# A hybrid encoder layer on one core: 192 instead of 128 tokens gathered, queries in two passes, one-hots in bf16

## The chip, the core and the metric

The kernel runs on one core of a Trainium2 chip. The metric is the device time of one execution in microseconds (us), lower is better. Engines are named as in the profile: PE is the matrix engine and PEld its weight loads, DVE the vector engine, ACT the scalar engine, POOL the GpSimd engine, SP the engine whose queue issues most loads. The core has 16 DMA engines that all queues share.

## What is computed

One layer over 512 tokens of width 2048: a normed input projection, two kinds of attention, an output projection with a residual, and then a channel mixer that retrieves single neurons. The change lies in the output projection's tail and in the mixer, which is, cut to what matters:

```python
qry = (xt @ w_query).reshape(T, 8, 2, 128)
sc = einsum('thcd,hckd->thck', qry, sub_keys)          # 2 x 128 scores per token and head
top_s, top_i = top_k(sc, 16)
cand_s = top_s[:, :, 0, :, None] + top_s[:, :, 1, None, :]
cand_i = top_i[:, :, 0, :, None] * 128 + top_i[:, :, 1, None, :]
best_s, best_pos = top_k(cand_s, 16)                   # 16 of 256 pairs
idx, gates = take(cand_i, best_pos), softmax(best_s)   # 8 heads x 16 = 128 neurons a token
act = gelu(sum_d(expert_down[idx] * xt))
out = sum_k(gates * act * expert_up[idx])              # 16384 neurons, rows of 2048 floats
```

## The kernel before

Tokens of the mixer are treated in two ways. For the first 384 (`DENSE`) all 16384 neurons are computed as matrix products, 128 groups `e` of 128 neurons, and the gates of the neurons not chosen are zero. For the other 128 tokens, one on each partition, the chosen rows of the two tables are gathered by indirect DMA, one row of 8 KB per token and slot, 128 slots for each table.

Every product in fp32 is made of three matmuls (`mm3`, lines 117 to 120): each operand is split into a high part (`high`, line 69, on ACT) and a rest (`low`, line 77, on DVE or, where the stream says so, on POOL). Weights come through `Stream`: loads of 1 MB on SP's queue, two raw buffers, each load cut into two pieces of 0.5 MB whose halves are made one piece ahead of the matmuls, into three buffers each.

The stages in order are: input projection and attention; the output projection (`out_granule`, line 582), four moving blocks of 384 columns and one of 512 per weight block; the query projection (line 923), eight heads, with two calls of `TopK` per head (lines 786 to 871) dealt out in four pieces each; a tail of 40 steps in which the first products of the mixer run beside the last top-k work; the one-hot stage (line 1043), 96 steps of 4 tokens, in which the gates are spread to a dense matrix: `e` compares (DVE), `eq` is one half times the gate (POOL in three of four steps, else DVE) and the other half copied by ACT, then four fp32 matmuls, then a copy, and the result goes to DRAM; some further products; and the dense stage (line 1176). There, 16 super-blocks of 8 groups `e` alternate between a down phase (two pieces per group) and an up phase (four column blocks `dc` of four pieces). I call a piece with its 24 matmuls a step; `after` (line 1148) is called once per step, 16 times in the first super-block, 26 times in the second and 32 times in each of the other 14, 490 times in all. It first moves the weighting of finished groups on by one operation (`Weighted.step`: a multiply by `rb2` out of PSUM, the gelu, the gate, the split) and then issues the gathers that are due: 257 items over 462 steps. An item is the fetch of the row two items on (POOL, line 1088, three buffers) and one DVE instruction on the row that has come: a multiply and sum in the first half (line 1096), a multiply and add in the second (line 1106). Each queue works in the order in which the program issues.

Of the kernel before, what the change touches and what calls it, by code (L numbers as in the profile page):

```python
# [21 lines left out]
S = 512  # L22
# [3 lines left out]
DENSE = 384  # L26
DB = DENSE // 128
# [70 lines left out]
def layer(ctx, tc, A, out_t, out_g):  # L98
# [107 lines left out]
    with ExitStack() as st:  # L206
# [268 lines left out]
        with ExitStack() as s2:  # L475
# [179 lines left out]
            o = [pj() for _ in range(5)]  # L655
# [10 lines left out]
    rb2 = gn.tile([128, DENSE], F32, name="rb2")  # L666
    rg = gn.tile([128, 1], F32, name="rg")
    xhl = pool(ctx, "xhl", side="right")
    yh = xhl.tile([128, NT, DENSE], F32R, name="yh")
    yl = xhl.tile([128, NT, DENSE], F32R, name="yl")  # L670
    sg = small.tile([128, 4], F32, name="sg", bufs=1)
    sq = small.tile([128, DENSE], F32, name="sq2", bufs=1)
    nc.gpsimd.dma_start(g2, A["g2"])
    tp2 = pool(out_stage, "tp2")
    xt, xg, x1 = {}, {}, {}

    def fetch(g):
        gs = slice(g * 512, (g + 1) * 512)
        xt[g] = tp2.tile([128, 4, DENSE], F32, name="xt2")
        nc.gpsimd.dma_start(xt[g], A["xT"][:, 4 * g:4 * g + 4, :DENSE])  # L680
        xg[g] = tp2.tile([128, 512], F32, name="xg"), tp2.tile([128, 512], F32, name="g2b")
        nc.gpsimd.dma_start(xg[g][0], A["xg"][:, gs])
        nc.gpsimd.dma_start(xg[g][1], A["g2r"][0:1, gs].to_broadcast([128, 512]))

    def residual(g, o):
        gs = slice(g * 512, (g + 1) * 512)
        x1[g] = tp2.tile([128, 4, DENSE], F32, name="x1")
        for c in range(4):
            nc.vector.tensor_tensor(x1[g][:, c, :], o[c][:, :DENSE], xt[g][:, c, :], op=OP.add)
# [9 lines left out]
    def scaled(dt):  # L699

        x = x1[dt // 4][:, dt % 4, :]
        nc.scalar.activation(yh[:, dt, :], x, AF.Copy, scale=g2[:, dt:dt + 1])
        q = sq if dt == 0 else tp2.tile([128, DENSE], F32, name="q2", bufs=2)
        nc.scalar.square(q, x)
        nc.vector.scalar_tensor_tensor(yl[:, dt, :], x, g2[:, dt:dt + 1], yh[:, dt, :].bitcast(F32),
                                       op0=OP.mult, op1=OP.subtract)
        if dt:
            nc.vector.tensor_tensor(sq, sq, q, op=OP.add)
# [3 lines left out]
    for g in range(1, 4):  # L712
        o = [pj() for _ in range(5)]
# [11 lines left out]
    slot = pool(ctx, "slot", side="right")  # L725
# [556 lines left out]
```

## Time and profile before

| | us |
|---|---|
| median of 3 runs (3424.23 to 3426.03) | 3425.71 |
| the profiled execution, its own time | 3424.43 |
| its span in the trace | 3422.7 |
| PE busy in the span | 3345.8 |
| DVE busy | 2288.5 |
| ACT busy | 1207.6 |
| POOL busy | 790.4 |

The profile gives for each engine its busy time, the instructions of each line with their mean duration, what they waited for, and the clock that PE was granted. Matmuls overlap each other, so the pace of matmuls is read from their starts and not from their durations. DMA is given as the mean busy share of the 16 engines and as GB/s.

### The profile page before, as it was taken

What the parts mean: (1) busy time and instruction counts of PE and PEld (TensorE: products, weight loads), DVE (VectorE), ACT (ScalarE), POOL (GpSimd) and SP (SyncE); (2) the same over time, 40 slices, a digit from 0 to 9 for tenths busy, and PEclk for the clock granted to TensorE, in tenths of its full rate; (3) what the DMA queues carried; (4) which work ended last, traced back from release to release, by engine and by line L of the source; (5) the groups of instructions that cost most, each with busy time, mean ns of one, the idle gap of its engine ahead of it and who ended that gap; (6) DMA issues with size and microseconds to landing.
All of it is one profiled execution on the core that took longest, in us unless ns stands there. A gap on an engine that the chain in (4) does not pass through costs nothing.

```text
span 3422.7 us, 46854 instructions
## 1 busy us (share of the span) xinstructions
PE 3345.8 (98%) x18845; PEld 3179.9 (93%) x18845; DVE 2288.5 (67%) x3660; ACT 1207.6 (35%) x1833; POOL 790.4 (23%) x670
## 2 busy tenths in 40 slices
PE   8999999999988789999999999999999999999999
PEld 6777878799988778999999999999999999999999
DVE  4545353553499996567777777767677777777675
ACT  4334444442222497323223223233232232232332
POOL 3112010100255573012222222222122222222220
PEclk9999999999999999999999999999999999999999
DMA  4222222233312245677777777777787777777775
GB/s 145 87 89 87 86 74 87 87 137 134 125 62 74 81 200 210 237 265 277 284 277 278 276 277 278 271 278 272 263 294 267 278 277 274 276 284 268 278 275 180
DMA packets 146379, 705.65 MB, mean 206 GB/s; under 512 B 11600, under 2 KB 61840, under 8 KB 68336
## 3 DMA queue, kind: packets, MB, share of 16 engines
q1 hardware_dynamic: 99552, 386.82, 32.0%
q0 software_dynamic: 40464, 283.32, 21.9%
q10 hardware_dynamic: 6144, 32.51, 2.4%
q8 instruction: 148, 2.42, 0.3%
q14 instruction: 71, 0.58, 0.1%
HBM read 665.90 MB, written 36.70 MB: 205 GB/s over the span
## 4 chain that ended last, share of the span: by engine, by line
PE 87%; DVE 7%; ACT 4%; issue 1%; DMA 0%; ACTq 0%; SPq 0%; DVEq 0%
PE pj L118 17%; PE pj L119 17%; PE pj L120 17%; PE pa L118 10%; PE pa L120 10%; PE pa L119 10%; ACT eq L1039 2%; PE pa L601 1%; PE pa L540 1%; ACT gs L109 1%; DVE sel L871 1%; PE pa L560 1%; PE pa L911 1%; DVE ti L803 0%; DVE ti L807 0%
## 5 line engine op out<-in xcount | busy, mean ns | idle before, releaser
L77 DVE TENSOR_TENSOR wl2x<-wr4x,wh2x 128x1024 fp32r<-128x1024 f32 x382 | 468.3, 1232 | 372.5 <-ACT wh2x L69 372.2
L118 PE MATMUL pj<-ah,wh2x 128*128 128x384 f32 x2048 | 684.3, 334 | 0.0
L119 PE MATMUL pj<-al,wh2x 128*128 128x384 f32 x2048 | 684.2, 334 | 0.0
L120 PE MATMUL pj<-ah,wl2x 128*128 128x384 f32 x2048 | 684.1, 334 | 0.0
L118 PE MATMUL pa<-yh,wh8x 128*128 128x384 f32 x2000 | 682.6, 341 | 0.0
L120 PE MATMUL pa<-yh,wl8x 128*128 128x384 f32 x2000 | 677.1, 339 | 0.0
L119 PE MATMUL pa<-yl,wh8x 128*128 128x384 f32 x2000 | 677.1, 339 | 0.0
L69 ACT CAST wh2x<-wr4x 128x1024 fp32r<-128x1024 f32 x382 | 400.6, 1049 | 708.7 <-PE pj L119 409.0
L77 DVE TENSOR_TENSOR wl8x<-wr16x,wh8x 128x1024 fp32r<-128x1024 f32 x254 | 312.7, 1234 | 152.8 <-ACT wh8x L69 152.3
L1088 POOL DMA_INDIRECT row<-in_down_dram,idx x128 | 207.2, 1619 | 831.2 <-DVE ga L1096 786.7
L119 PEld LDWEIGHTS pj<-al,wh2x 128*128 128x128 f32 x2048 | 384.4, 188 | 0.0
L120 PEld LDWEIGHTS pj<-ah,wl2x 128*128 128x128 f32 x2048 | 384.4, 188 | 0.0
L118 PEld LDWEIGHTS pj<-ah,wh2x 128*128 128x128 f32 x2048 | 384.4, 188 | 0.0
L1088 POOL DMA_INDIRECT row<-in_up_dram,idx x128 | 207.5, 1621 | 764.2 <-DVE xn L1106 728.8
L118 PEld LDWEIGHTS pa<-yh,wh8x 128*128 128x128 f32 x2000 | 375.5, 188 | 0.0
L119 PEld LDWEIGHTS pa<-yl,wh8x 128*128 128x128 f32 x2000 | 375.5, 188 | 0.0
L120 PEld LDWEIGHTS pa<-yh,wl8x 128*128 128x128 f32 x2000 | 375.3, 188 | 0.1
L69 ACT CAST wh8x<-wr16x 128x1024 fp32r<-128x1024 f32 x256 | 267.0, 1044 | 190.4 <-PE pj L119 81.6
L1200 DVE TENSOR_TENSOR x<-x,pj 128x384 f32<-128x384 f32 x256 | 141.9, 554 | 257.2 <-PE pj L120 257.1
L1106 DVE SCALAR_TENSOR_TENSOR xn<-row,ga,xn 128x2048 f32<-128x2048 f32 x127 | 297.8, 2345 | 0.0
L1096 DVE CUSTOM_DVE_ANT_0 row<-row,xn 128x2048 f32<-128x2048 f32 x128 | 292.3, 2284 | 0.0
L118 PE MATMUL pj<-wh2x,xh 128*128 128x512 f32 x704 | 284.1, 404 | 0.0
(300 smaller groups left out, 4777.3 us busy)
## 6 DMA issues: line engine op xcount, KB each, us to landing
wr16x<-in_downT_dram SPq DMA_DIRECT2D x128, 1024.0 KB, 5.1
wr4x<-in_upT_dram SPq DMA_DIRECT2D x128, 1024.0 KB, 5.5
wr4x<-in_win_dram SPq DMA_DIRECT2D x47, 1024.0 KB, 4.9
gt_d<-gs ACTq DMA_DIRECT2D x12, 2048.0 KB, 6.5
g<-gt_d SPq DMA_DIRECT2D x30, 768.0 KB, 8.6
wr4x<-in_wout_dram SPq DMA_DIRECT2D x16, 1024.0 KB, 4.9
wr8x<-in_wq_dram SPq DMA_DIRECT2D x16, 1024.0 KB, 5.0
xt<-in_xT_dram SPq DMA_DIRECT2D x7, 512.0 KB, 8.5
```

The source lines that it names most:

```text
L69: self.nc.scalar.copy(hi, t)
L77: self.lo_engine[n].tensor_tensor(lo, t, hi.bitcast(F32), op=OP.subtract)
L109: nc.scalar.copy(out, in_)
L118: nc.tensor.matmul(out, sh, mh, start=first, stop=False)
L119: nc.tensor.matmul(out, sh, ml, start=False, stop=False)
L120: nc.tensor.matmul(out, sl, mh, start=False, stop=last)
L540: nc.tensor.matmul(sc[u], qt[:, h, t * 128:(t + 1) * 128], kt[:, h, :], start=True, stop=True)
L1039: nc.scalar.copy(eq[:, 1].rearrange("p t k -> p k t"), e[:, 1])
L1088: nc.gpsimd.indirect_dma_start(out=t, out_offset=None, in_=A["down"] if step < SLOTS else A["up"], in_offset=bass.IndirectOffsetOnAxis(ap= ...
L1096: nc.vector.tensor_tensor_reduce(t, t, xn, 1.0, 0.0, OP.mult, OP.add, ga[:, k:k + 1])
L1106: nc.vector.scalar_tensor_tensor(xn, t, ga[:, k:k + 1], xn, op0=OP.mult, op1=OP.add)
L1200: nc.vector.tensor_tensor(x1[:, dt, :], x1[:, dt, :], o[c], op=OP.add)
```

## The change

The gathered tokens become 192 (`NG`), the dense ones 320. Of the gathered ones, 128 lie one on a partition as before (b = 0); the other 64 are laid on 128 partitions as halves of the width (b = 1): rows of 4 KB, half a table row each, and the two half sums are added by a small matmul (`weights_of_slots`) before the gelu. The gather items become 514, b = 0 and b = 1 in turn, over the same 462 steps. The rests of the weights of the dense stage are made by POOL for 2 pieces of 5 (`lo_share`), by DVE for the others. The norm factor `rb2` moves from the products of each group (line 1126, dropped) into the dense input (`dense_y`); the residual `x1` stays in SBUF and no longer goes through DRAM. The output projection runs with all 512 columns as moving. The queries run in two passes over the same weights, which are loaded and split twice: first the 192 gathered tokens (192 moving columns), then the 320 dense ones; the number of top-k calls stays at 16, four or two heads or token groups packed in one. The last scaling of a top-k call moves from DVE to ACT, the sums of squares from DVE to POOL. In the one-hot stage, now 80 steps, the gate is split in three bf16 parts and the matmuls are 12 in bf16 instead of 4 in fp32; ACT's copy `eq` is dropped, and one `w` of 1536 elements takes the place of an `eq` of 512, on POOL in one of three steps. The diff, cut to its core:

```diff
-DENSE = 384
-DB = DENSE // 128
+NG = 192
+DENSE = S - NG
...
-    for k in range(8):
+    for k in range(16):
         for a in range(0, NT, 8):
-            ws.add(A["wq"][k, :, a:a + 8, :], 2, (nc.gpsimd, nc.gpsimd if k == 0 else None))
+            ws.add(A["wq"][k % 8, :, a:a + 8, :], 2, (nc.gpsimd,))
...
-                        mm3(o[c][:, :DENSE], wh[:, a, cs], wl[:, a, cs], mh[k][:, kk, :DENSE], ml[k][:, kk, :DENSE],
-                            f, l)
-                    mm3(o[4], mh[k][:, kk, DENSE:], ml[k][:, kk, DENSE:], wh[:, a, :], wl[:, a, :], f, l)
+                        mm3(o[c], wh[:, a, cs], wl[:, a, cs], mh[k][:, kk, :], ml[k][:, kk, :], f, l)
...
-        nc.scalar.dma_start(x1_d[:, 4 * g:4 * g + 4, :], x1[g])
+            dt = 4 * g + c
+            nc.vector.tensor_tensor(xq[:, dt, :], o[c][:, DENSE:], xt[g][:, c, DENSE:], op=OP.add)
+            nc.vector.tensor_tensor(x1[:, dt, :], o[c][:, :DENSE], xt[g][:, c, :DENSE], op=OP.add)
...
+        nc.scalar.square(q[:, DENSE:], xq[:, dt, :])
+        nc.scalar.square(q[:, :DENSE], x1[:, dt, :])
...
-            nc.vector.tensor_tensor(sq, sq, q, op=OP.add)
+            nc.gpsimd.tensor_tensor(sq, sq, q, op=OP.add)
...
+
+    def lo_share():
+
+        shares[0] += 1
+        return nc.gpsimd if shares[0] % 5 in (1, 3) else None
...
-        ws.add(A["downT"][e], 2, (nc.gpsimd if e in (1, 2) else None,))
+        ws.add(A["downT"][e], 2, (lo_share(), lo_share()) if e >= PRE else (nc.gpsimd if e in (1, 2) else None,))
...
-                ws.add(A["upT"][sb, dc, :, e:e + 4, :])
+                ws.add(A["upT"][sb, dc, :, e:e + 4, :], 2, (lo_share(), lo_share()))
...
+        def dense_y(dt):
+
+            t = qp.tile([128, DENSE], F32, name="yt", bufs=2)
+            nc.vector.scalar_tensor_tensor(t, x1[:, dt, :], g2[:, dt:dt + 1], rb2[:, :DENSE], op0=OP.mult, op1=OP.mult)
+            nc.scalar.copy(yh[:, dt, :], t)
+            nc.gpsimd.tensor_tensor(yl[:, dt, :], t, yh[:, dt, :].bitcast(F32), op=OP.subtract)
...
-                    nc.vector.tensor_scalar(ge, ge, sm[:, 3 * h + 2:3 * h + 3], None, op0=OP.mult)
+                    nc.scalar.activation(ge, ge, AF.Copy, scale=sm[:, 3 * h + 2:3 * h + 3])
...
+                        mm3(o[c][:, :NG], w[0][:, a, cs], w[1][:, a, cs], zh[:, dt, :], zl[:, dt, :], dt == 0, dt == NT - 1)
...
+                if 1 <= h < 7 and q % 2 == 0 and h * 2 + q // 2 - 2 < 6:
+                    turned_x(h * 2 + q // 2 - 2)
+                if h and q != 1 and (h - 1) * 3 + (q + 1) // 2 < NT:
+                    dense_y((h - 1) * 3 + (q + 1) // 2)
+                pieces(1)
...
+                        mm3(o[c][:, :DENSE], w[0][:, a, cs], w[1][:, a, cs], yh[:, dt, :], yl[:, dt, :], dt == 0, dt == NT - 1)
+                    if q == 0 and a == 1:
+                        scored.one()
+                if q == 0:
+                    scored.two()
+                pieces(2 if q % 2 else 1)
...
-            if n in (7, 12, 20, 28):
+            if n in (7, 12, 18, 22, 26, 30):
...
-            eq = eqs[n] = gp.tile([128, 2, 4, 128], F32, name="eq", bufs=4)
-            (nc.vector if n % 4 == 3 else nc.gpsimd).tensor_tensor(
-                eq[:, 0].rearrange("p t k -> p k t"), e[:, 0], gd[:, ts].unsqueeze(1).to_broadcast([128, 128, 4]), op=OP.mult)
-            nc.scalar.copy(eq[:, 1].rearrange("p t k -> p k t"), e[:, 1])
+            w = gp.tile([128, 3, 128, 4], BF16, name="w", bufs=4)
+            (nc.gpsimd if n % 3 == 2 else nc.vector).tensor_tensor(
+                w, e[:, 0].unsqueeze(1).to_broadcast([128, 3, 128, 4]),
+                gd[:, :, ts].unsqueeze(2).to_broadcast([128, 3, 128, 4]), op=OP.mult)
...
-                nc.tensor.matmul(b[:, u, :], eq[:, 1, u, :], eq[:, 0, u, :], start=True, stop=True)
+                for k in range(3):
+                    nc.tensor.matmul(b[:, u, :], e[:, 1, :, u], w[:, k, :, u], start=k == 0, stop=k == 2)
...
+            fetched[b, step] = t = rows.tile([128, width[b]], F32, name=f"row{b}", bufs=3)
...
+                src = halves[up] if b else A["up" if up else "down"]
+                nc.gpsimd.indirect_dma_start(out=t, out_offset=None, in_=src,
+                                             in_offset=bass.IndirectOffsetOnAxis(ap=idx[b][:, k:k + 1], axis=0))
...
+    def gather(b, step):
+        fetch_rows(b, step + 2)
         k = step % SLOTS
-        t = fetched.pop(step)
...
+            nc.vector.tensor_tensor_reduce(t, t, x, 1.0, 0.0, OP.mult, OP.add, g[:, k:k + 1])
...
+            nc.vector.scalar_tensor_tensor(x, t, g[:, k:k + 1], x, op0=OP.mult, op1=OP.add)
...
-                if self.a is None:
-                    self.a = prep.tile([128, DENSE], F32, name=f"pre{self.e % E}")
-                    nc.vector.tensor_tensor(self.a, self.bank, rb2, op=OP.mult)
-                nc.scalar.activation(self.a, self.a, AF.Gelu_apprx_tanh)
+                src = self.a
+                if src is None:
+                    self.a, src = prep.tile([128, DENSE], F32, name=f"pre{self.e % E}"), self.bank
...
-        while gathered[0] < min(2 * SLOTS + 1, (steps[0] - 16) * 2 * SLOTS // total):
-            gather(gathered[0])
+        if wait_slots[0]:
+            wait_slots[0] -= 1
+            if wait_slots[0] == 0:
+                weights_of_slots()
+            return
+        while gathered[0] < min(END, (steps[0] - 16) * END // total):
+            step, b = divmod(gathered[0], 2)
+            gather(b, step)
             gathered[0] += 1
+            if gathered[0] == 2 * SLOTS:
+                wait_slots[0] = 2
+                return
...
```

## Rows read from the trace of the kernel before

**Rows 1.** The page's first part: busy time, share of span, instructions.
```profile
PE 3345.8 (98%) x18845; PEld 3179.9 (93%) x18845; DVE 2288.5 (67%) x3660; ACT 1207.6 (35%) x1833; POOL 790.4 (23%) x670
```
**Rows 2.** Busy time by stage: length, then engines, granted clock, DMA share, GB/s.
```profile
720.00:889.00 169.00, 169.00 (x916) 160.85 (x915) 59.95 (x73) 48.55 (x67) 9.69 (x11) 1.00 0.39 136
889.00:1131.00 242.00, 216.47 (x1330) 211.99 (x1328) 212.00 (x930) 59.17 (x130) 121.15 (x99) 0.95 0.24 79
1131.00:1167.00 36.00, 27.75 (x145) 27.16 (x146) 33.81 (x145) 9.03 (x24) 17.06 (x15) 0.86 0.27 88
1167.00:1325.00 158.00, 134.25 (x961) 120.90 (x960) 144.34 (x141) 146.33 (x202) 110.83 (x77) 0.98 0.43 174
1361.00:3420.00 2059.00, 2058.15 (x11764) 2057.71 (x11762) 1471.14 (x1503) 617.46 (x738) 415.88 (x258) 1.00 0.74 270
```
**Rows 3.** PE in order of time in the query stage: start, duration, line, shape.
```profile
953.65 0.28 PE L118 MATMUL pj<-wh4x,gh 128*128 128x256 f32 x1
954.97 0.28 PE L120 MATMUL pj<-wh4x,gl 128*128 128x256 f32 x1
```
**Rows 4.** Costliest groups of DVE, POOL and ACT in the dense stage, by form.
```profile
L77 DVE TENSOR_TENSOR wl2x<-wr4x,wh2x 128x1024 fp32r<-128x1024 f32 x255 | 309.2, 1222 | 105.8 <-ACT wh2x L69 105.6
L1106 DVE SCALAR_TENSOR_TENSOR xn<-row,ga,xn 128x2048 f32<-128x2048 f32 x127 | 297.8, 2345 | 0.0
L1096 DVE CUSTOM_DVE_ANT_0 row<-row,xn 128x2048 f32<-128x2048 f32 x128 | 292.3, 2284 | 0.0
L69 ACT CAST wh2x<-wr4x 128x1024 fp32r<-128x1024 f32 x254 | 266.7, 1050 | 575.5 <-PE pj L119 396.1 <-DMA wr4x<-in_upT_dram 120.7 <-DVE wl2x L77 29.3
L1088 POOL DMA_INDIRECT row<-in_up_dram,idx x128 | 207.5, 1621 | 764.2 <-DVE xn L1106 728.8 <-DVE ga L1096 17.2 <-DVE xn L1104 7.1
L1200 DVE TENSOR_TENSOR x<-x,pj 128x384 f32<-128x384 f32 x256 | 141.9, 554 | 257.2 <-PE pj L120 257.1
L1130 DVE TENSOR_TENSOR pre<-pre,g 128x384 f32<-128x384 f32 x125 | 69.0, 552 | 0.0
L1126 DVE TENSOR_TENSOR pre<-pa,rb 128x384 f32<-128x384 f32 x120 | 66.9, 557 | 85.4 <-PE pa L120 85.1
```
**Rows 5.** DMA in 1500 to 3000 us by queue, and two short stretches by windows.
```profile
q1 hardware_dynamic: 59776, 203.96, 38.3%
q0 software_dynamic: 28484, 207.40, 36.1%
...
1780.00:1790.00 10.00, 10.00 (x60) 10.00 (x59) 6.75 (x11) 2.11 (x2) 2.64 (x2) 1.00 1.00 413
2620.00:2640.00 20.00, 20.00 (x116) 20.00 (x115) 15.27 (x15) 7.21 (x10) 5.05 (x3) 1.00 0.94 363
```
**Rows 6.** DVE and POOL in order of time, where their tensor instructions meet.
```profile
1143.42 2.40 POOL L77 TENSOR_TENSOR wl8x<-wr16x,wh8x 128x1024 fp32r<-128x1024 f32 x1 [4.74 <-ACT wh8x L69]
1144.32 2.58 DVE L77 TENSOR_TENSOR wl8x<-wr16x,wh8x 128x1024 fp32r<-128x1024 f32 x1 [0.34 <-ACT wh8x L69]
...
1210.99 1.10 POOL L1037 TENSOR_TENSOR eq<-e,gd 128x512 f32<-128x512 bf16 x1 [1.42 <-DVE e L1034]
1229.09 0.68 DVE L1034 TENSOR_TENSOR e<-ij,io 128x1024 bf16<-128x1024 bf16 x1
1229.69 1.21 DVE L77 TENSOR_TENSOR wl8x<-wr16x,wh8x 128x1024 fp32r<-128x1024 f32 x1
1229.91 1.94 POOL L1037 TENSOR_TENSOR eq<-e,gd 128x512 f32<-128x512 bf16 x1 [1.53 <-DVE e L1034]
1230.82 0.55 DVE L983 TENSOR_TENSOR pre<-pa,rb 128x384 f32<-128x384 f32 x1
```
**Rows 7.** Groups of the top-k work and of POOL's rests, by form, whole span.
```profile
L871 DVE TENSOR_SCALAR sel<-sel,smk 128x16 f32<-128x16 f32 x32 | 50.4, 1575 | 1.1
L77 POOL TENSOR_TENSOR wl4x<-wr8x,wh4x 128x1024 fp32r<-128x1024 f32 x18 | 43.1, 2393 | 96.6 <-ACT wh4x L69 96.6
L859 POOL TENSOR_TENSOR oh<-eqa,tf 128x1024 f32<-128x1024 bf16 x16 | 32.3, 2017 | 53.0 <-DVE smk L870 44.8 <-DVE eqa L856 6.7 <-issue 1.5
```

More of the change, by code (lines that the diff above doesn't have):

```diff
@@ L654, in layer @@
             turn(us[3])
-            o = [pj() for _ in range(5)]
+            o = [pj() for _ in range(4)]
             for q in range(8):
@@ L712, in layer @@
     for g in range(1, 4):
-        o = [pj() for _ in range(5)]
+        o = [pj() for _ in range(4)]
         for q in range(8):
@@ L877, in pieces, with queue @@
                 todo.pop(0)()
-        def queue(t, h, sc):
-            k = TopK(t, h, sc)
+        def queue(dst, sc, then=None):
+            k = TopK(dst, sc)
             def last():
@@ new lines, in packed_scores @@
+        def packed_scores(sel, h, qt, sk):
+            hp, i = h % 2, h // 2
+            rows = slice(64 * hp, 64 * hp + 64)
+            if h % 4 == 0:
+                packed[id(sel)] = qp.tile([128, 4, NK], F32, name="scp")
+            sc = packed[id(sel)]
+            b = pa()
+            for c in range(2):
+                nc.tensor.matmul(b[rows, c * 128:(c + 1) * 128], qt[:, c, :], sk[:, c, :], start=True, stop=True)
+            m = 2 * (i % 2)
+            copy(sc[rows, m:m + 2, :].rearrange("p a b -> p (a b)"), b[rows, :256])
+            if h % 4 == 3:
+                queue(units(sel, i - 1), sc)
@@ L907, in pair, with two, __init__, one @@
+            def two(self):
+                packed_scores(sel_b, self.h, self.qt[:, :, 0:64], self.sk)
+        class DenseScores:
+            def __init__(self, h, o):
+                self.h, self.sk = h, keys(h)
+                self.qt = qp.tile([128, 2, DENSE], F32, name="qT", bufs=2)
+                for c in range(2):
+                    copy(self.qt[:, c, :], o[c][:, :DENSE])
+            def one(self):
                 b = pa()
@@ new lines, in layer @@
+        gstack.close()
+        slot = pool(ctx, "slot", side="right")
+        idx = [slot.tile([128, SLOTS], I32, name=f"idx{b}") for b in range(2)]
+        gate = [slot.tile([128, SLOTS], F32, name=f"gate{b}") for b in range(2)]
+        ga = [slot.tile([128, SLOTS], F32, name=f"ga{b}") for b in range(2)]
+        qm = slot.tile([128, 128], F32, name="qm")
+        prep = pool(ctx, "prep", side="right")
+        for h in range(8):
+            o = [pj(), pj()]
+            for q in range(4):
+                w = ws.next()
+                for a in range(4):
+                    dt = 4 * q + a
+                    for c in range(2):
+                        cs = slice(c * 128, c * 128 + 128)
+                        mm3(o[c][:, :DENSE], w[0][:, a, cs], w[1][:, a, cs], yh[:, dt, :], yl[:, dt, :], dt == 0, dt == NT - 1)
+                    if q == 0 and a == 1:
+                        scored.one()
+                if q == 0:
+                    scored.two()
+                pieces(2 if q % 2 else 1)
+            scored = DenseScores(h, o)
@@ L1209, in layer @@
                 after()
-    assert gathered[0] == 2 * SLOTS + 1 and not pipe
+    assert gathered[0] == END and not pipe
 def _lay_out(i):
```

350 lines of the change are left out of this document (194 added, 156 removed).

## The prediction

> **What bounds the kernel now.** I read the busy times first: PE is busy for 98% of the span and DVE for 67% [rows 1]. Then the stages [rows 2], because an average hides that they have different limits. The dense stage is 2059 of the 3422.7 us, PE is busy in all of it at the full granted clock (1.00, the 2.4 GHz level), and DVE is busy for 1471 us, 71%. So there the number of matmuls times their pace sets the time, and DVE waits for ACT and PE [rows 4]. The query stage (889 to 1131 us) is different: PE has gaps, the granted clock averages 0.95, and DVE is busy for 212 of 242 us; DVE's top-k work ends last. So it is in the tail (33.8 of 36 us). In the one-hot stage DVE, ACT and POOL are all far in (144, 146, 111 of 158 us).
>
> Next come two views that show resources which PE's waits don't. The DMA engines are at 0.74 and 270 GB/s in the dense stage [rows 2]; their best 10 us read 413 GB/s at a share of 1.00, and one of the best stretches of 20 us 363 GB/s at 0.94 [rows 5]. And DVE and POOL don't run freely beside each other [rows 6]. A rest on DVE takes 1.21 us; where POOL had 1.50 us of its own rest still to do it took 2.58, that is 1.37 more. POOL's `eq` takes 1.10 us alone; begun while a DVE rest had 0.99 us to go it took 1.94. The DVE instruction that reads one operand from PSUM (line 983) took its 0.55 us beside POOL. So a DVE instruction with two operands in SBUF and a tensor instruction on POOL take turns, and each POOL one costs DVE nearly its whole length.
>
> **The change, dense stage.** A step is 24 matmuls; 490 steps are 11760 matmuls, and 2059/11760 is 175 ns each, 4.20 us a step. With 256 columns twelve starts from 953.65 to 954.97 us lie 1.32/11 = 120 ns apart [rows 3]. 320 columns lie halfway: 147.5 ns, 3.54 us a step. Were PE still the bound, the stage would take 1735 us, 324 less. That a shorter matmul gives nothing is excluded by those 120 ns. What is late next:
>
> DVE, per super-block of 32 steps. There are 32 rests; POOL takes 2 of 5, so 19.2 x 1.222 us = 23.5. There are 514/462 x 32 = 35.6 gather items, half of them whole rows at (2.284 + 2.345)/2 = 2.315 us: 17.8 x 2.315 = 41.2. Half rows: 552 ns at 384 elements and 2345 at 2048 make 1.08 ns an element, so 1024 elements less are 1.10 us less: 17.8 x 1.21 = 21.5. The gate and split, 16 x (552 - 69) ns = 7.7; the sums into `x1`, 16 x (554 - 69) ns = 7.8; the multiply by `rb2` (8 x 557 ns) is gone [rows 4]. Sum 101.7. Neighbours overlap a little: in the dense stage the groups' times of before add to 1547 us and DVE is busy for 1471, a factor 0.95. So 96.7 us, 3.02 a step, and alone this would hide under PE. But POOL's 12.8 rests of 2.393 us [rows 7] block it. By rows 6 a block costs the length less some 0.3 us: 12.8 x 2.1 = 27. Together 123.6 us, 3.86 a step, more than PE's 3.54. From below: what meets a sum into `x1` (an operand in PSUM) or a time when DVE waits anyway costs nothing; with none of it costing, DVE is at 3.02 and PE is the bound.
>
> DMA, per step: 0.524 MB of weights, 1.1126 x 0.786 MB of rows, 0.041 MB of gates, 1.44 MB in all. At 413 GB/s that is 3.49 us. From the other side: the two queues' 38.3% and 36.1% [rows 5] of 4.2 us are 3.12; gathers move 207.40 MB in 36.1% of 1500 us, 383 GB/s, so 0.29 MB of half rows add 0.76 and fewer gates take off 0.04: 3.84 us.
>
> POOL: 1.1126 x 1.62 us of issuing [rows 4] and 0.4 x 2.39, 2.76 us a step; it hides, though each issue still waits for the DVE instruction that frees its buffer, and a rest queued behind it waits too.
>
> So three servers stand at 3.54, 3.49 to 3.84, and 3.02 to 3.86, linked by few buffers: halves one piece ahead, gathers two items ahead, DVE in order behind rows that must have landed and sums that wait for PE (257 us of idle before line 1200, which cost nothing before). Nothing in this trace shows what the links cost when all are full. I take DVE's upper end, as rows 6 are direct, and 0.09 us for the links (about 3 us a super-block, an idle of 0.7 us at each of the four groups of sums): 3.95 us a step, 490 x 3.95 = 1936, **-123 us**. The combination of the half sums, in which PE waits once for DVE, is some 2 us and inside this.
>
> The Trainium skill's page "SBUF — State Buffer" (on the port pair shared by VectorE and GpSimd) states the turn-taking as an exclusive lock held for the whole instruction. The trace agrees: the 1.37 us above. By this rule the step would be 3.86, by the busy times without it 3.54.
>
> The page "HBM Reference" of the Trainium skill gives some 425 GB/s for a core that streams alone. 413 GB/s in 10 us is near it, but no stretch of 20 us shows it. By that figure DMA would need 3.39 us a step and never bind.
>
> **The other stages.** The output projection has 12 matmuls of 512 columns per weight block for 12 of 384 and 3 of 512: by the slope of 0.43 ns a column about 12 x 0.23 against 12 x 0.175 + 3 x 0.23, so 64 x 0.03 = 2 us less, and with the DRAM writes gone I take -4 (bounds -6 to +6, as the new sums of squares run on POOL).
>
> Queries: the matmul work goes from 384 columns at 175 ns and 256 at 120 ns, 768 x 0.175 + 384 x 0.120 = 180 us, to 768 x 0.1475 plus 768 of 192 columns, not shown; between the slope's 92 ns and the 120 ns of 256 columns, so 185 to 205 us. DVE was the bound, with 16 top-k calls; their last scaling, 50.4 us over 32 [rows 7], goes to ACT. That takes some 45 us off. Against it: all 32 pieces of weights are split a second time, half of the rests on POOL, 16 dense splits come in with a POOL part, and PE and DVE now peak in different passes. A top-k call costs DVE some 10 us: 212 us less some 30 of rests and multiplies over 14 calls is 13, less the 3.1 of the scaling. Pass one: 96 x 0.107 + 1.2 = 11.5 us of PE a head, which waits for DVE's multiply before the scores of the head before; some 16 us. Pass two: 1.5 top-k calls of 10 us and two rests a head, 17.5 us. 8 x 33.5 = 268 against 242: **+26** (0 to +70).
>
> Tail: three calls instead of two are left over, and everything must be finished before the first one-hot, where a third of it came 12 steps into the loop: +10 and +4, so **+14** (0 to +25).
>
> One-hots: before, DVE and POOL in turns explain the pace: `e` 0.57, a quarter of 1.06, three quarters of 0.95, and rests 0.1 make 1.6 us, and 158/96 is 1.65. Now per step: `e` 0.57, two thirds of a `w` on DVE (1536 elements in the same form as `e`, which needs 0.68 for 1024 [rows 6]: 0.85 net), one third of a `w` on POOL (2.02 us for 1024 [rows 7], so about 3.0, 2.85 net), rests 0.11: 2.2 us, x 80 = 176, **+18** (from -10, were `w` on POOL at `eq`'s 1.1 us, to +45 at 3.6 us and PE's 12 matmuls on top). The products between the stages, four groups of 48 matmuls at 27 ns less: -5.
>
> Sum: -4 + 26 + 14 + 18 - 5 - 123 = -74. The profiled execution's 3424.4 us lies 1.3 under the median of 3425.7, which is less than anything here; so **3350 us**.
>
> **The rivals.** (a) POOL's rests fall into times when DVE waits anyway, and DMA runs near 413 GB/s. For it: DVE idles 106 us before the up phase's rests now [rows 4]. Against it: that idle exists since PE is the bound. Then a step is PE's 3.54 plus 0.1: 490 x 3.64 = 1784, and 3424 + 49 - 275 = 3198. (b) The other side: rows land late, and DVE, in order, holds back the rests that PE needs. Place: the wait before lines 1096 and 1106, where there is none now. At 3.84 us of DMA and a share of 0.90 in place of 1.00 a step takes 4.27 us: 2092, and 3424 + 49 + 33 = 3506. It decides from 4.10 us a step, a share of 0.937. For it: no 20 us above 0.94 so far; against it: four items are in flight where two were, so the queue seldom runs dry. (c) The front costs its upper bounds, 140 us, and the dense stage gains as forecast: 3441.
>
> **How the numbers follow.** Forecast 0.45, (a) 0.25, (b) 0.22, (c) 0.08. The range reaches into (a) and (b): 3215 to 3490. Faster by over 0.2% (7 us, about what a measurement can tell from no change): most of the forecast and (a), 0.70; within 0.2%: 0.05; slower: the rest of the forecast, (b) and (c), 0.25.
>
> **What would show it.** The starts of 320-column matmuls 147 ns apart; PE with gaps in the dense stage, ended by DVE or POOL rests; DVE's rests and row instructions longer than 1.22 and 2.3 us where POOL makes a rest; DMA share 0.9 or more. If PE stays without gaps there, (a) holds. If DVE waits for rows, (b). The forecast would be wrong most of all if blocks and waits add rather than overlap, since then each tenth of a us a step is 49 us.

## The result, and the profile after

The changed kernel takes **3523.02 us** (median of 4 runs, 3521.72 to 3541.61) where the kernel before takes 3425.07 (4 runs): a ratio of 1.0299, 95% interval 1.0264 to 1.0333. It is 3% slower; the forecast was 3350 us, 2.2% faster. The profiled execution took 3524.16 us, its span is 3522.1. Times given below without a range are single executions; the changed kernel's own four lie 20 us apart, so the small differences are read from the stages and not from the totals.

First the stages, which answer to [rows 2]. The columns are the stretch, its length, busy time of PE, PEld, DVE, ACT and POOL with their instructions, then the granted clock of PE, the DMA share and GB/s.

```profile
720.00:888.00 168.00, 168.00 (x754) 139.53 (x754) 65.26 (x76) 49.13 (x78) 18.84 (x16) 1.00 0.33 116
888.00:1093.00 205.00, 133.03 (x891) 126.05 (x891) 105.83 (x310) 54.52 (x102) 91.96 (x78) 0.74 0.30 100
1093.00:1287.00 194.00, 142.19 (x865) 132.51 (x863) 125.74 (x628) 54.43 (x122) 95.04 (x78) 0.89 0.27 91
1287.00:1335.00 48.00, 26.47 (x155) 24.45 (x154) 27.48 (x135) 12.62 (x35) 22.94 (x26) 0.75 0.22 76
1335.00:1510.00 175.00, 151.30 (x1145) 140.64 (x1144) 172.96 (x147) 56.69 (x95) 81.58 (x26) 0.90 0.33 133
1510.00:1544.00 34.00, 33.30 (x232) 32.63 (x230) 14.93 (x15) 13.73 (x19) 4.39 (x3) 1.00 0.63 225
1544.00:3519.00 1975.00, 1804.05 (x11762) 1754.22 (x11761) 1753.17 (x1574) 598.77 (x742) 1430.13 (x711) 0.98 0.91 347
```

| stage | before | after | measured | forecast |
|---|---|---|---|---|
| output projection | 169 | 168 | -1 | -4 |
| queries (pass one 205, pass two 194) | 242 | 399 | **+157** | **+26** |
| tail | 36 | 48 | +12 | +14 |
| one-hots | 158 | 175 | +17 | +18 |
| products between | 36 | 34 | -2 | -5 |
| dense | 2059 | 1975 | **-84** | **-123** |
| sum | | | +99 | -74 |

3424.4 + 99 is 3523, the time measured, so no loss is hidden elsewhere. 131 of the 173 us between forecast and result lie in the query stage, 39 in the dense stage. In the query stage no engine is busy for more than 74% of either pass, and PE's granted clock is 0.74 and 0.89: everybody waits. What PE waits for there (times are total, count, longest):

```profile
PE pj L120 <- POOL wl4x L77: 44.3, 19, 6.6
PE pa L957 <- DMA sk<-in_subk_dram: 38.3, 5, 9.9
PE pa L979 <- DMA sk<-in_subk_dram: 27.3, 7, 10.0
PE pa L957 <- DVE ti L832: 10.5, 1, 10.5
PE pj L118 <- ACT wh4x L69: 3.2, 6, 0.6
```

There are two main names: the rests of the weights on POOL, and `sk`, the keys against which a head's scores are taken. Before, the keys came in one load of 1 MB at the start of the stage. Now the constructors of the two scores classes ask for 128 KB per head with `keys(h)`, on POOL's queue, when the head's matmuls have been issued; PE needs them a few matmuls into the next head. One such place in pass two, POOL and PE in order of time (start, length, engine, line; in brackets the idle time before it):

```profile
1132.71 2.01 POOL L884 TENSOR_TENSOR oh<-eqa,tf 128x1024 bf16<-128x1024 bf16 x1 [1.63 <-DVE smk L895]
1134.80 3.26 POOL L888 TENSOR_TENSOR oh<-oh 128x512 bf16<-128x512 bf16 x3
1138.14 0.30 POOL L890 TENSOR_TENSOR sel_d<-oh 128x64 f32<-128x64 bf16 x1
1138.62 0.58 POOL L920 DMA_DIRECT2D sk<-in_subk_dram  x1 [0.18 <-issue]
...
1142.65 2.05 PE L979 MATMUL pa<-sk,qT 128*128 128x128 f32 x8 [10.00 <-DMA sk<-in_subk_dram]
```

PE was done with the matmuls before at 1132.65. The request stood behind 5.6 us of top-k work in POOL's queue, went out at 1138.62 and the keys were used 4.0 us later: PE stood still for 10 us.

The dense stage shows both candidates of the forecast at once: DVE and POOL in turns, and DMA. The rests of DVE and POOL and DVE's row operations are longer than in [rows 4] and [rows 7], and ACT waits for weights. PE's longest waits there are for the rests, 101 us for POOL's and 40 for DVE's. The groups of DVE, POOL and ACT by form (busy, mean ns | idle before, by releaser):

```profile
L1236 DVE SCALAR_TENSOR_TENSOR xn<-row,ga,xn 128x2048 f32<-128x2048 f32 x127 | 340.8, 2684 | 3.1 <-DMA row<-in_up_dram,idx 3.1
L1229 DVE CUSTOM_DVE_ANT_0 row<-row,xn 128x2048 f32<-128x2048 f32 x128 | 324.0, 2531 | 4.7 <-DMA row<-in_down_dram,idx 4.7
L77 DVE TENSOR_TENSOR wl2x<-wr4x,wh2x 128x1024 fp32r<-128x1024 f32 x153 | 209.9, 1374 | 72.3 <-ACT wh2x L69 70.2 <-PE pa L120 1.9
...
L77 POOL TENSOR_TENSOR wl8x<-wr16x,wh8x 128x1024 fp32r<-128x1024 f32 x93 | 286.5, 3080 | 184.4 <-ACT wh8x L69 179.2 <-PE pj L120 4.7
...
L69 ACT CAST wh2x<-wr4x 128x1024 fp32r<-128x1024 f32 x255 | 263.1, 1051 | 564.7 <-DMA wr4x<-in_upT_dram 373.9 <-PE pj L119 129.9 <-PE pj L120 33.6
```

### The profile page after: what moved, and what is told of

Same layout as the page of the kernel before. It is cut to its first block, busy times and chain, and to the rows that moved or that the text cites. A ratio compares the mean times of both kernels' runs of the same rounds, so it can differ in the third digit from the quotient of the medians.

```text
span 3522.1 us, 48635 instructions
## 1 busy us (share of the span) xinstructions
PE 3162.4 (90%) x19300; PEld 2913.5 (83%) x19300; DVE 2617.1 (74%) x3736; ACT 1151.8 (33%) x1843; POOL 1857.6 (53%) x1144
## 4 chain that ended last, share of the span: by engine, by line
DVE 19%; PE 17%; DMA 14%; issue 9%; POOL 9%; ACT 2%; POOLq 0%; DVEq 0%; ACTq 0%; SPq 0%
DMA wr16x<-in_downT_dram 7%; DMA wr4x<-in_upT_dram 5%; PE pj L120 4%; PE pj L118 4%; PE pj L119 4%; DVE row L1229 3%; POOL wl8x L77 3%; DVE xn L1236 2%; POOL row L1213 2%; DVE wl8x L77 2%; DVE wl2x L77 2%; DVE w L1167 2%; PE pa L120 2%; POOL wl2x L77 2%; PE pa L118 2%
## 5 line engine op out<-in xcount | busy, mean ns | idle before, releaser
L120 PE MATMUL pa<-yh,wl8x 128*128 128x320 f32 x2000 | 636.6, 318 | 85.0 <-POOL wl8x L77 67.7
L120 PE MATMUL pj<-ah,wl2x 128*128 128x320 f32 x2048 | 646.9, 316 | 58.0 <-POOL wl2x L77 33.5
L118 PE MATMUL pj<-ah,wh2x 128*128 128x320 f32 x2048 | 640.2, 313 | 13.4 <-ACT wh2x L69 12.2
L118 PE MATMUL pa<-yh,wh8x 128*128 128x320 f32 x2000 | 635.1, 318 | 14.9 <-ACT wh8x L69 14.8
L119 PE MATMUL pj<-al,wh2x 128*128 128x320 f32 x2048 | 638.4, 312 | 0.1
L119 PE MATMUL pa<-yl,wh8x 128*128 128x320 f32 x2000 | 626.8, 313 | 0.0
L1213 POOL DMA_INDIRECT row<-in_down_dram,idx x256 | 433.6, 1694 | 83.5 <-issue 41.7
L1213 POOL DMA_INDIRECT row<-in_up_dram,idx x256 | 426.2, 1665 | 76.4 <-issue 39.1
L118 PEld LDWEIGHTS pa<-yh,wh8x 128*128 128x128 f32 x2000 | 384.9, 192 | 17.5 <-ACT wh8x L69 17.4
L77 POOL TENSOR_TENSOR wl8x<-wr16x,wh8x 128x1024 fp32r<-128x1024 f32 x95 | 291.2, 3065 | 193.4 <-ACT wh8x L69 188.2
L77 POOL TENSOR_TENSOR wl2x<-wr4x,wh2x 128x1024 fp32r<-128x1024 f32 x103 | 284.0, 2757 | 195.8 <-ACT wh2x L69 182.6
L1236 DVE SCALAR_TENSOR_TENSOR xn<-row,ga,xn 128x2048 f32<-128x2048 f32 x127 | 340.8, 2684 | 3.1 <-DMA row<-in_up_dram,idx 3.1
L1229 DVE CUSTOM_DVE_ANT_0 row<-row,xn 128x2048 f32<-128x2048 f32 x128 | 324.0, 2531 | 4.7 <-DMA row<-in_down_dram,idx 4.7
```

The source lines that it names most:

```text
L77: self.lo_engine[n].tensor_tensor(lo, t, hi.bitcast(F32), op=OP.subtract)
L118: nc.tensor.matmul(out, sh, mh, start=first, stop=False)
L119: nc.tensor.matmul(out, sh, ml, start=False, stop=False)
L120: nc.tensor.matmul(out, sl, mh, start=False, stop=last)
L1213: nc.gpsimd.indirect_dma_start(out=t, out_offset=None, in_=src, in_offset=bass.IndirectOffsetOnAxis(ap=idx[b][:, k:k + 1], axis=0))
L1229: nc.vector.tensor_tensor_reduce(t, t, x, 1.0, 0.0, OP.mult, OP.add, g[:, k:k + 1])
```

## Experiments on the query stage

In the expectations a granule is a piece with its matmuls.

**Keys a head earlier.**

```diff
+        coming = [keys(0)]
+        def next_keys(h):
+            coming.append(keys((h + 1) % 8))
+            return coming.pop(0)
...
-                self.h, self.sk = h, keys(h)
+                self.h, self.sk = h, next_keys(h)
```

> The changed kernel with one edit: the 128 KB of keys of a head (sk) are requested one head earlier, when the scores of the head before are set up, so that they have a whole head (about 25 us) to arrive. Nothing else moves. Of after, the query stage lasts 399 us (888 to 1287), the whole 3523. Theory K (the keys stand behind POOL's rests and gain rows in POOL's in-order queue and then take some 5 us to land, PE stands still for them 12 times, and its granted clock drops after it): the waits of lines 957 and 979 for sk (65.6 us in all) go to under 10, the stage to 290 to 335 us, the whole to 3400 to 3460. Rival P (PE waits for POOL's rests of the weights and the top-k work anyway, the keys are only what is seen last): the stage stays above 370, PE's wait moves to the rests wl4x and to DVE, the whole to 3495 to 3515.

Measured: 3463.44 us (3452.43 to 3468.77), ratio to the kernel before 1.0113 (1.0089 to 1.0138). The two passes, in the columns used above:

```profile
888.00:1054.00 166.00, 129.05 (x893) 122.75 (x893) 103.93 (x312) 54.06 (x100) 91.79 (x79) 0.83 0.38 124
1054.00:1228.00 174.00, 140.50 (x859) 131.90 (x859) 122.11 (x628) 53.93 (x121) 94.13 (x78) 0.91 0.31 100
```

The stage takes 340 instead of 399, no other stage moves by more than 8. PE's waits there are now:

```profile
PE pj L120 <- POOL wl4x L77: 58.8, 21, 6.7
PE pj L118 <- ACT wh4x L69: 6.0, 7, 2.7
PE pa L963 <- DVE qg L954: 3.0, 3, 1.6
```

Theory K holds: the waits for `sk` are gone, and so is the single wait of 10.5 us that the profile put down to DVE's `ti`; the keys cost 59 us. The stage (340) and the total (3463) both lie just above its ranges, as the rests on POOL remain.

**POOL's queue cleared, and no rests on POOL in pass two.** On top of the first edit, gain rows and `yl` are issued when what they wait for is done; the rests of pass two go to DVE.

```diff
-            ws.add(A["wq"][k % 8, :, a:a + 8, :], 2, (nc.gpsimd,))
+            ws.add(A["wq"][k % 8, :, a:a + 8, :], 2, (nc.gpsimd if k < 8 else None,))
...
-            if k + 2 < 6:
-                gain_rows(k + 2)
...
+                if 1 <= h < 7 and q % 2 and h * 2 + q // 2 < 6:
+                    gain_rows(h * 2 + q // 2)
...
+            rest_of_y()
```

> As e1_keys_ahead (keys a head earlier), and in pass one POOL's loads of the gain rows and its rests of the dense input (yl) are issued one granule or more later, when what they wait for is done, so that the rests of the weights don't stand behind a POOL instruction that waits; in pass two the rests of the weights are all on DVE. In e1_keys_ahead pass one took 166 us with 28 us of PE waiting for POOL's rests, pass two 174 with 31. Theory Q (in-order queue: what POOL waits for delays the rests behind it): pass one 140 to 155, pass two 145 to 160. Rival W (POOL's own work, turns with DVE and the halved clock set the pace, not the waits): both within 8 us of e1_keys_ahead; with DVE as the bound pass two may even grow to 185.

Measured: 3444.01 us; pass one 167 us (no change), pass two 160 (174), with the clock at 0.98 there. Pass one:

```profile
886.00:1053.00 167.00, 128.21 (x894) 121.61 (x893) 109.48 (x312) 54.33 (x102) 94.14 (x78) 0.83 0.38 125
```

Half of theory Q fell: what waits in front of the rests in POOL's queue was not what pass one lost. A place in its pass one shows the rest itself:

```profile
962.90 1.99 ACT L69 CAST wh4x<-wr8x 128x1024 fp32r<-128x1024 f32 x2
964.02 2.35 POOL L77 TENSOR_TENSOR wl4x<-wr8x,wh4x 128x1024 fp32r<-128x1024 f32 x1 [1.87 <-ACT wh4x L69]
966.42 0.53 PE L120 MATMUL pj<-zh,wl4x 128*128 128x192 f32 x1 [1.96 <-POOL wl4x L77]
...
969.53 0.41 PE L119 MATMUL pj<-zl,wh4x 128*128 128x192 f32 x1
969.74 0.41 PE L120 MATMUL pj<-zh,wl4x 128*128 128x192 f32 x1
...
973.40 0.27 PE L120 MATMUL pj<-zh,wl4x 128*128 128x192 f32 x1
973.51 0.27 PE L118 MATMUL pj<-zh,wh4x 128*128 128x192 f32 x1
```

Two things are to be seen. POOL begins the rest as soon as ACT has the high part, and its 2.35 us are still too late for PE. And after the wait PE runs at the halved clock, matmuls 0.21 us apart, until it is back at 0.11. So pass one could be slow through the clock or through the rest. Two runs ask which it is.

**The clock held up by added work.**

```diff
                 w = ws.next()
+                for _ in range(12):
+                    nc.tensor.matmul(jk[:, :NG], zh[:, 0, 0:128], zh[:, 1, :], start=True, stop=True)
```

> As q3_pool_late_dve2, with 12 matmuls of 192 columns added ahead of each of the 32 granules of pass one; they read only the high parts of the input, wait for nothing but the matmuls before them, and write to a bank that nobody reads. Pass one of q3_pool_late_dve2: 167 us, granted clock 0.83, PE idle for 38 us, the matmuls 110 ns apart at the full clock and 213 at the halved one. The added ones are 32 x 12 x 0.110 = 42 us at the full clock, 82 at the halved one. Theory C (the halved clock after each gap is what pass one loses): the clock stays at 0.95 or above and pass one takes 140 to 158 us in spite of the added work. Rival L (the chain from ACT's high part over POOL's rest sets the pace, the clock only follows): the clock rises, pass one stays at 160 to 172. Rival W (PE's work sets it): 195 or more.

**The rests on POOL left out in pass one.**

```diff
+        if self.lo_engine[n] is self.nc.gpsimd and (a, b) == (4, 256):
+            self.split[n] = hi, hi
```

> As q3_pool_late_dve2, but in pass one the 16 rests of the weights on POOL are left out, and the matmuls read the high part in their place (so these queries are not the right ones). Pass one of q3_pool_late_dve2: 167 us, PE waiting 26.8 us in it for these rests. Theory L (POOL's rest of 2.35 us, behind ACT's high part of 1.04, is longer than a granule's 2.7 us of matmuls, so with one piece of lead PE waits for it, and the clock falls): pass one 125 to 145 us, clock 0.92 or more. Rival C (the clock stays low because of the other gaps): 150 to 165.

Pass one of the first, then of the second:

```profile
886.00:1048.00 162.00, 154.35 (x1278) 150.07 (x1276) 108.37 (x312) 54.34 (x101) 94.81 (x78) 0.94 0.39 128
```
```profile
886.00:1005.00 119.00, 105.37 (x894) 100.96 (x892) 83.40 (x312) 54.16 (x101) 56.46 (x63) 0.97 0.53 173
```

With 384 added matmuls the clock is 0.94 in place of 0.83 and the pass takes 162 us in place of 167. That is inside rival L's range, but PE is now busy for 154 of the 162 us, so the added work takes up most of what the clock gave back, and this run alone can't price the clock. The second run decides. Without the 16 rests the pass takes 119 us: the rests on POOL are the cause, and with them gone the clock is 0.97. (Left out is more than moved: in best3, below, DVE makes nearly all of them and the pass takes 143.) Of the 48 us, 25 were PE's idle time (39 before, 14 now), and 23 lie in the same 894 instructions of PE, busy for 105 us in place of 128. So the low clock came with the waits, and it made them about twice as dear.

Part of the reason can be read from the rows: a piece's 24 matmuls of 192 columns last 24 x 0.11 = 2.7 us; ACT's high part (1.04) and POOL's rest (2.35) need 3.4, and they run only one piece ahead. In the kernel before, the same piece carried 24 matmuls of 384 columns and 12 of 256, by [rows 2, 3] 24 x 0.175 + 12 x 0.12 = 5.6 us, and covered them. But 0.7 us at 16 rests are 11 us, and PE waited 26.8 for them in pass one of q3. In the place above ACT started late as well: it had stood 1.39 us for DVE's `yt` before the copy `yh` at 962.54, and made the high parts of two pieces right behind it. How the wait divides between the chain and such late starts is not shown.

## Experiments on the dense stage

Four runs free one of the two candidates, or both. Each is the changed kernel with the edit named, cut to its core; d2, d3 and d4 leave work out.

```diff
 d1: -        return nc.gpsimd if shares[0] % 5 in (1, 3) else None
     +        return None
 d2: +        if b and step < 2 * SLOTS:
     +            t, x = t[:, :64], x[:, :64]
 d3: +        if b and 2 <= step < 2 * SLOTS:
     +            fetched[b, step] = kept[step % 2]
     +            return
 d4: d1 and d3
```

> The changed kernel, but all rests of the weights of the dense stage are made by DVE (after has 2 pieces of 5 on POOL). The dense stage of after lasts 1975.5 us (4.03 us a step), PE waits 101 us in it for rests on POOL and 40 for rests on DVE. Theory T (DVE and POOL taking turns sets the step): DVE's rests fall back from 1.33-1.47 us to 1.22, the row operations from 2.5-2.7 to 2.3, DVE's sum is about 32 x 1.22 + 41.2 + 21.5 + 15.5 = 117 us a super-block less the 5% of overlap = 111, 3.5 a step, so the stage comes to 1800 to 1890 us. Rival D (DMA sets it: weights land late at a share of 0.91): the stage stays at 1920 to 1985, DMA share 0.91 or more, and PE waits for the high parts (ACT, behind the weight DMA) instead.

> The changed kernel, but the product-and-sum and the product-and-add on the half rows (b = 1, 256 instructions) work on 64 of their 1024 columns only; the rest of these sums is left out of the computation. All DMAs stay. It takes some 256 x 1.1 = 280 us off DVE in the dense stage (1975.5 us in after). Theory T (DVE and POOL in turns set the step): stage 1750 to 1830 us. Rival D (DMA sets it): stage 1920 to 1985, DVE's busy share down to 0.76 and DMA still at 0.91.

> The changed kernel, but the half rows (b = 1) are fetched only for the first two slots and used again for all others, so that 252 of 257 x 0.52 MB fetches fall away; the sums of these 64 tokens are left out of what is computed rightly, all DVE instructions on them stay. It takes some 130 MB, about a fifth of the bytes, off the dense stage, and 252 issues of 1.68 us off POOL. Theory T (DVE and POOL in turns set the step): the stage stays at 1930 to 1985 us, DMA share about 0.73. Rival D (DMA sets it): stage 1740 to 1850.

> The changed kernel with two edits of the dense stage together: all rests of its weights on DVE, and half rows (b = 1) fetched for the first two slots only (the sums of these 64 tokens are left out of what is computed rightly, their DVE work stays). One at a time the stage went from 1975 us to 1928 (rests on DVE, DMA share 0.98) and to 1943 (few fetches, DVE busy for 1763 us of it). Theory S (two bounds side by side, DMA on one side and the turn-taking of DVE and POOL on the other, each right behind the other): with both away DVE needs some 111 us a super-block, 3.5 a step, about PE's 3.54, and the stage comes to 1750 to 1830 us, far more than the 47 + 32 of the two alone. Rival L (the chain of a piece from its load over ACT and the rest to PE, with two load buffers, sets the step whatever the servers do): the gains only add, 1880 to 1910 us.

The dense stage of d1, d2, d3 and d4:

```profile
1545.00:3473.00 1928.00, 1798.15 (x11762) 1751.04 (x11760) 1655.35 (x1770) 593.30 (x743) 815.40 (x510) 0.98 0.92 354
```
```profile
1539.00:3505.00 1966.00, 1807.86 (x11765) 1769.07 (x11764) 1457.97 (x1575) 601.02 (x742) 1360.97 (x711) 0.97 0.90 348
```
```profile
1542.00:3485.00 1943.00, 1792.00 (x11759) 1755.14 (x11758) 1763.31 (x1573) 597.67 (x742) 1010.54 (x457) 0.98 0.78 284
```
```profile
1547.00:3330.00 1783.00, 1749.42 (x11765) 1726.76 (x11763) 1652.71 (x1770) 596.68 (x743) 442.52 (x257) 1.00 0.84 308
```

(The 0.98 that the expectation of d4 gives as d1's DMA share is its clock; the share is 0.92.) The five other runs that leave the dense stage as it is (e1, q3, c1, c2 and h1, below) took 1968 to 1988 us for it, so the 1975 of the changed kernel is known to some 10 us.

From 1975 us, d1 takes off 47 and d3 32, together they take off 192. Neither T nor D was right alone: two bounds stand side by side, and whoever frees one meets the other 32 to 47 us below. d2 makes it plainest: 295 us less of DVE's time and 9 us gained, which is no more than the scatter, as DMA (0.90) and POOL's rests stay. In d1 DVE's rests take 1221 ns and its full rows 2347 and 2286 (1374, 2684 and 2531 with POOL's rests beside them), so the turns of [rows 6] were real:

```profile
L77 DVE TENSOR_TENSOR wl2x<-wr4x,wh2x 128x1024 fp32r<-128x1024 f32 x255 | 310.9, 1221 | 109.9 <-ACT wh2x L69 109.6
```

What they cost DVE can be estimated from its busy time: 1753 us, less d1's 1655 without the 195 rests that POOL makes in the changed kernel (195 x 1.22 = 238), leaves 336 us, or 1.7 us for each rest on POOL. Two things stay joined in these runs. d1 and d4 take away the turns and also POOL's late rests, for which PE waited 101 us. And d3 and d4 take away DMA work and also 420 us of POOL's issuing. The half loads below answer the second: with all issues in place the stage comes to 1823 us. The first is open.

d1's DMA share is 0.92 and not 1.00. Why does it stop there? **Loads of half the size, into twice as many buffers of the same memory.** It was tried on the repaired kernel (below), on the changed one and on the one before.

```diff
-            self.piece.append((len(self.loads), k * n, n))
+            self.piece.append((len(self.loads), 0, n))
...
-        self.loads.append(src)
+            self.loads.append(src[:, k * n:(k + 1) * n, :])
...
-    ws = Stream(nc, wp, "w", 2, 3, 1)
+    ws = Stream(nc, wp, "w", 4, 3, 1)
```

> The changed kernel with one edit: loads of 0.5 MB into four buffers in place of 1 MB into two, as in l1_half_loads; POOL keeps 2 rests of 5. Dense stage of after 1975 us. Theory B+T (the load link and the turn-taking are two bounds of about the same height, so freeing one alone leaves the other): DVE with POOL stays at the 1943 us that it needed with most half rows not fetched, so the stage comes to 1925 to 1960 us, the whole to 3475 to 3510. Rival B (the load link alone is the loss): 1830 to 1890 us. The query stage stays within 10 us of 399 in both.

> The kernel before with the same edit of the loads alone. Its dense stage (2059 us) had PE busy for 2058 us at the full clock, so a fuller DMA queue can't shorten it: stage 2055 to 2062 us, the whole 3415 to 3428. Were the link a loss in the kernel before too, the whole would fall below 3405, and what l1_half_loads gained would not belong to the change.

Measured: the changed kernel 3510.2 us, the one before 3426.32 beside 3426.33 without the edit. Their dense stages:

```profile
1550.00:3505.00 1955.00, 1805.11 (x11763) 1769.94 (x11761) 1763.22 (x1573) 593.14 (x739) 1437.25 (x711) 0.97 0.94 350
```
```profile
1361.00:3420.00 2059.00, 2059.00 (x11770) 2058.88 (x11769) 1471.07 (x1502) 617.81 (x739) 417.93 (x258) 1.00 0.76 270
```

The 1955 us are at the upper end of B+T's range, only 13 below the lowest of the six runs with this stage unchanged; rival B (1830 to 1890) is excluded. The kernel before has no such loss: PE was its bound. The whole picture of the dense stage in us (the last cell of the middle row is from l1, below):

| | POOL makes 2 rests of 5 | DVE makes all |
|---|---|---|
| loads of 1 MB, two buffers | 1975 | 1928 (d1) |
| loads of 0.5 MB, four buffers | 1955 (l2) | 1823 (l1) |
| 1 MB, few half rows fetched | 1943 (d3) | 1783 (d4) |

## The one-hots, and the parts together

**Every `w` on DVE.**

```diff
-            (nc.gpsimd if n % 3 == 2 else nc.vector).tensor_tensor(
+            nc.vector.tensor_tensor(
```

> The changed kernel, but in the one-hot stage every w is made by DVE (in after each third one by POOL). In after a w takes POOL 3.1 us, a w on DVE 0.96 us alone and 3.39 beside POOL's, and the stage (first e to last e) 174.6 us with DVE busy for 173. Theory T (turn-taking makes the stage): DVE then needs 80 x (0.65 + 0.96) + 10 for rests = 139 us, PE 80 x 12 x 0.113 + 27 = 136; the stage comes to 142 to 158 us, the whole to some 3495 to 3505. Rival B (DVE's 27 more w cost it what POOL's turns cost now, or PE at its lower clock is the bound): 168 to 190.

Measured: 3496.07 us, the one-hot stage 139 in place of 175, below theory T's 142:

```profile
1335.00:1474.00 139.00, 139.00 (x1121) 130.78 (x1120) 134.79 (x172) 55.33 (x93) 0.00 (x0) 1.00 0.42 167
```

PE is now busy in all of it, at the full clock, and DVE for 134.8 us, so PE has become the bound. The turn-taking in the changed kernel, DVE and then POOL in the same few us:

```profile
1400.74 3.39 DVE L1167 TENSOR_TENSOR w<-e,gd 128x1536 bf16<-128x1536 bf16 x1
1404.06 0.68 DVE L1164 TENSOR_TENSOR e<-ij,io 128x1024 bf16<-128x1024 bf16 x1
1404.77 0.96 DVE L1167 TENSOR_TENSOR w<-e,gd 128x1536 bf16<-128x1536 bf16 x1
```
```profile
1400.25 3.07 POOL L1167 TENSOR_TENSOR w<-e,gd 128x1536 bf16<-128x1536 bf16 x1 [3.15 <-DVE e L1164]
```

POOL's `w` ended at 1403.32 and DVE's at 1404.13, 0.8 us later, nearly its own 0.96 after POOL was done. A third of the work on POOL made the stage a quarter longer. The Trainium skill's page "SBUF — State Buffer" (section "SBUF: two separate sides") describes a lock held for the whole instruction; these rows agree.

**All repairs.** best1 joins the edits of q3, d1 and h1; best3 also moves the rests of pass one to DVE, but for one head (`nc.gpsimd if k == 5`); l1 is best3 with the half loads.

> All repairs at once, everything computed: keys a head earlier, POOL's gain rows and yl issued later, rests of pass two and of the dense stage on DVE, all w of the one-hots on DVE. If the parts add: 3523 - 60 (keys) - 47 (dense rests) - 25 (w) - 30 (POOL's queue) = 3361 us, range 3335 to 3400, below the 3425 of the kernel before. If the parts share one cause: above 3415.

> As best1, and in pass one the rests of the weights are on DVE too, but for the fifth of the eight heads counted from zero, whose first halves stay on POOL. Everything is computed. Theory L (with 192 columns a granule is too short to hide a rest on POOL: without those rests pass one took 119 us in c2_no_pool_rest, with them 165): DVE gets 14 x 1.22 = 17 us more and loses the turns, pass one takes 122 to 140 us, the whole 3362 - 33 = 3330 (3320 to 3340). Rival D (DVE, with the top-k work, gains and inputs in front of the rests in its own order, becomes what PE waits for): pass one 150 or more, the whole 3350 or more.

> As best3, but the weights come in loads of 0.5 MB (one piece each) into four buffers, where it was loads of 1 MB (two pieces) into two, so the same memory; a new load can start whenever one piece is split, not only after every second. Everything is computed. In best3 the dense stage takes 1938 us at a DMA share of 0.91, PE waits there for the high and low parts, and ACT for weights that have not landed. Theory B (the share stays under 1 because the two load buffers are the link that runs empty): the share rises to 0.94 or more, the stage falls to 1860 to 1910 us, the whole to 3270 to 3320. Rival M (0.91 is what weights and gathers together get from the DMA engines, whatever the order): the stage stays within 1920 to 1950 us, the whole within 3335 to 3360.

| | us (range of the runs) | ratio to the kernel before | pass one | pass two | one-hots | dense |
|---|---|---|---|---|---|---|
| best1 | 3362.48 (3353.24 to 3366.20) | 0.9812 (0.9794 to 0.9830) | 164 | 160 | 139 | 1930 |
| best3 | 3347.34 (3317.35 to 3354.79) | 0.9748 (0.9698 to 0.9798) | 143 | 162 | 139 | 1938 |
| l1 | 3232.38 (3226.48 to 3237.22) | 0.9435 (0.9419 to 0.9451) | 144 | 163 | 139 | 1823 |

best1 came within 2 us of the 3361 expected. The gains of its parts as measured one by one (79 for q3, 46 for d1, 27 for h1) add to 3371, 9 us more than it took, so the causes are nearly separate. In best3 pass one falls between the two expectations: PE's wait for POOL's rests there is down to 3 us, 11 us of waiting for DVE's have come. The dense stage of best3, then of l1:

```profile
1408.00:3346.00 1938.00, 1808.48 (x11760) 1759.89 (x11759) 1654.57 (x1770) 593.91 (x744) 811.56 (x510) 0.97 0.91 352
```
```profile
1408.00:3231.00 1823.00, 1766.03 (x11765) 1741.56 (x11763) 1652.37 (x1768) 596.25 (x741) 895.28 (x510) 0.99 0.97 374
```

In l1 the DMA share rises to 0.97 and 374 GB/s and the dense stage gains 115 us, more than theory B asked for; ACT waits 374 us for weights that have not landed where it waited 813 in best3. Whether the smaller transfer does it, or the buffer that comes free one piece earlier, no run tells apart. So the change as made costs 98 us, and the kernel with these edits around it gains 192. Of the edits only the half loads were tried on the kernel before; what the others would give it is open.

One page of the Trainium skill speaks against that last edit: "DMA: Bandwidth & Descriptors", section "Measured (HBM→SBUF, 128 partitions, SWDGE, issued from GpSimd)", asks for transfers of 1 MiB or more to get 75% of the peak, as measured on transfers that GpSimd issues. Here the weights come on SP's queue, and 0.5 MB in four buffers moved 374 GB/s where 1 MB in two moved 352; the measurement decides, and it compares loads at a fixed memory, which that section does not.

## Why the prediction was wrong, step by step

- **The bound before** was right: PE, at the full clock, in the dense stage. The half loads change nothing there.
- **Queries, +26 forecast, +157 measured. This step failed**, in two places. The load of the keys was not in the sum at all: the prediction counted what is split twice and which engine does it, but not the key requests that the two constructors put into POOL's queue, behind its rests and top-k work (59 us). And the rests on POOL were priced as time of DVE and POOL, with "some 16 us" and "17.5 us" a head from engine sums, and not as something that PE waits for: left out, they give back 48 us in pass one (24 with DVE making nearly all of them), and moved to DVE 14 in pass two. With 192 columns a piece (2.7 us) no longer covers the 3.4 us of the next one's high part and rest. With 320 it lasts 24 x 0.147 = 3.5 us and just covers them, and how the 14 us divide between POOL's queue and the turns with DVE, no run shows. With keys and rests away the passes take 119 and 160 us, 279; the forecast's 268 was the time of a stage whose waits are hidden. With the rests of pass one made, but nearly all on DVE, it is 143 and 162 us, 305, a cost of 63. The upper bound of +70, for which the prediction gives no working, did not hold the result either.
- **The clock.** The prediction took the pace of the full clock for the queries; 0.74 and 0.89 were granted. In pass one that is no cause of its own, as the clock came back when the rests went, but it doubled the price of the waits: 23 of the 48 us.
- **Dense, -123 forecast, -84 measured.** The mechanism was right in the main, as the signs that the prediction named all came (320 columns 147 ns apart, PE's gaps ended by rests, longer rests and rows, a DMA share of 0.91). With DMA freed, DVE and POOL in turns give 1943/490 = 3.97 us a step where 3.95 was forecast, but that nearness is partly luck: DVE was busy for 1763/490 = 3.60 of it and not for 3.86, as a rest on POOL cost it 1.7 us by the estimate above and not 2.1, and the waits were 0.37 and not the 0.09 of the links. With both freed a step takes 3.64, which is the figure of rival (a). Mis-sized were the term for the links and DMA's place under it: with the turns freed and two load buffers a step takes 1938/490 = 3.96 us, with four half-size buffers 3.72. So the link of the two load buffers is worth some 0.23 us by itself, and DMA stood level with the turns instead of below them.
- **Rival (b)** named rows that land late as the way to a slower kernel. That did not occur: DVE waited 9 us for rows in the whole stage. What landed late were the weights: ACT waited 374 us for the up weights, where before it was 121 [rows 4]. The result is on the slower side through the front (all stages ahead of the dense one), as in rival (c), but 183 us and not its 140: its bounds were too low for the queries.
- **One-hots, tail, products, output projection** were within 3 us each. The step of the one-hots, 2.2 us forecast, is 175/80 = 2.19, and h1 took away the turns that it was built from.

## What to carry to other kernels

When a matmul gets narrower, go through everything that was hidden under the wide one: a piece's chain (load, high part, rest) needs a cover as long as itself, and a rest on a slow engine can lose it first. Count every DMA request that an edit moves, and read what stands before it in the queue of the engine that issues it. Where two servers end near each other, free both before judging either: here 47 and 32 us alone were 192 together.

## What the runs showed that was not expected

- The size and number of the loads mattered at equal memory: DMA share 0.91 and 352 GB/s with two buffers of 1 MB, 0.97 and 374 with four of 0.5 MB.
- PE paid for its waits twice: without the rests on POOL, pass one lost 25 us of PE's idle time and 23 us of its busy time for the same matmuls, as the granted clock rose from 0.83 to 0.97.
- Kernels in which PE waits spread more from run to run here: 3521.72 to 3541.61 for the changed one and 3317.35 to 3354.79 for best3, against 3423.64 to 3425.90 for the kernel before beside it.
